# Forgetting attention with its queries, keys, decay and maxima as 16-bit pieces in place of 32-bit ones

## The chip, the cores and the metric

The program runs on 1 core of one Trainium2 chip. The metric is device microseconds (us) of one execution; the time before is the median of 3 runs. A profiled execution is a further run, with a trace of every engine. Engines: PE (TensorE matmul), PEld (its weight loads), DVE (VectorE), ACT (ScalarE), POOL (GpSimd), SP (SyncE, which issues the DMAs).

## The reference

One layer: RMS norm, one input projection, two groups of heads (native sparse attention, NSA, and forgetting attention, FoX), gates, one output projection. There is a prompt of 1024 tokens and a decode batch of 8 x 8 tokens with paged caches. The change touches FoX on the prompt:

```python
def fox_core(q, cq, q_pos, k, v, ck, k_pos):
    s = jnp.einsum('bqhd,bkhd->bhqk', q, k).astype(jnp.float32) * (HEAD_DIM ** -0.5)
    s = s + (jnp.transpose(cq, (0, 2, 1))[:, :, :, None] - jnp.transpose(ck, (0, 2, 1))[:, :, None, :])
    p = masked_softmax(s, k_pos[None, :] <= q_pos[:, None])
    return jnp.einsum('bhqk,bkhd->bqhd', p.astype(v.dtype), v)
```

There are 8 heads of 64. q and k are RMS normed with gains, and c is the running sum of log-forget values over the tokens, so that a score is q.k/8 + c[query] - c[key]. A row's own c[query] falls out of its softmax, so the kernel adds -c[key] alone.

## The kernel before

**Stages.** Prompt tokens are worked in 8 tiles of 128. From 0 to about 366 us the input projection runs chunk after chunk (11 chunks of 256 or so columns, `project`, L237 and L244: 24 matmuls of 128x256 per tile, on 16-bit halves of the input and the weights), with the compression branch, the decay and the operands of FoX head 0 put in as background work at fixed chunks (chunk 6 `nsa_scales`, chunk 8 `fox_decay`, chunk 9 `fox_first`). From 366 us FoX runs over 8 heads, and the last 4 chunks of the projection (36 tiles, kinds `z`) are its filler: after each key block of FoX a quota of 0.48 tiles is let in, until head 6 has had its first half. The second half of head 6 and head 7 run after that, at a raised priority, beside the first loads of the NSA stage and of the decode batch. NSA, the decode batch and the output projection follow.

**FoX on one head h** (buffers of two, i = h % 2):
- `fox_prep(h)`: loads k and q, splits each into a part hi (ACT, L663, rounded to a 32-bit format of TensorE called fp32r) and lo (POOL, L664), transposes both on PE (L669, groups of four 128x128 with `ident`), and copies them out of PSUM (k1 on ACT, L690; q1 on DVE, L693). k1 holds hi over lo, q1 holds lo over hi; the hi halves go by DMA (L694, L695) to rows 0 to 63 of km and qm. Rows 64 and 65 of km hold the decay in two rows (from `cpark`, L685), and qm has ones there.
- `fox_max(h, c)`: row maxima of the scores of one half c of the queries: qm against km over 66 rows (L757), reduced on DVE with the causal mask (L744) or without (L762), into `mst`. `put_max` then transposes the 4 columns of maxima on PE (L722) and writes them, shifted and with a minus, into rows 96 to 99 of qm (DVE, L723), each in its own block of columns.
- `fox_attend(h, c)`: for each key block the score is two matmuls into one PSUM bank (st, two banks): km x qm over 100 rows (L774: hi.hi, decay, minus the maximum) and k1 x q1 over 128 rows (L775: hi.lo and lo.hi). A mask matmul follows on the diagonal (L777). `exp_split` takes exp on ACT (L702, to pf), a 16-bit hi of it on ACT (L705, phi) and the rest lo on DVE, or each fifth time on POOL (L707, plo). `pv` multiplies with the values (L715 to L717), three short matmuls a block of 128 queries.

NSA already works on 16-bit halves: its scores are L1107 and L1108, its exp is L1112 with a bias and a scale read from the tile `nsc`, and its maxima go by `put_max16` (two scaled 16-bit rows each, L732 and L733, one transpose L735, one write L736).

**What sets the order.** A scheduler puts the instructions of each engine in one fixed order when the program is built; each engine then runs its own list in order and waits on semaphores. DMAs are issued by SP in its order.

Of the kernel before, what the change touches and what calls it, by code (L numbers as in the profile page):

```python
# [30 lines left out]
QSCALE = 2.0 ** 10  # L31
TINY = 1e-30
# [55 lines left out]
def bc(ap, shape):  # L88
    return ap.to_broadcast(shape)
# [3 lines left out]
def layer_kernel(ctx, tc, a, o):  # L93
# [15 lines left out]
    nsc = P.tile([128, 8], F32, name="nsc")  # L109
# [7 lines left out]
    gains = P.tile([128, 6, 64], F32, name="gains")  # L117
# [136 lines left out]
    def heads(ap, h):  # L254
        return ap.rearrange("p (h d) -> p h d", h=h)
# [363 lines left out]
    cpark = nc.dram_tensor("cpark", (2, 8, T), F32).ap()  # L619
    km, qm, k1, q1 = [], [], [], []  # L620

    def fox_operands(pool, tags):
        for r, n, tag in zip((km, qm, k1, q1), ("km", "qm", "k1", "q1"), tags):
            r.append(pool.tile([128, T], F32R, name=f"{n}{len(r)}", tag=tag))
        e = nc.gpsimd if pool is C else nc.vector
        e.memset(km[-1][64:96].bitcast(F32), 0.0)
        e.memset(km[-1][96:128].bitcast(F32), 1.0)
        e.memset(qm[-1][64:96].bitcast(F32), 1.0)

    def fox_decay():  # L630
        tri = C.tile([128, 128], F32, name="tri")
        nc.sync.dma_start(tri, a["c_tri"][:, 0:128])
        pc = PS.tile([128, NT, 8], F32, name="ctr", bufs=1)
        nc.tensor.matmul(pc, tri, logf[:, 0:NT], start=True, stop=False)
        for j in range(NT - 1):
            nc.tensor.matmul(pc[:, j + 1:], ones, bc(logf[:, j:j + 1], [128, NT - 1 - j, 8]),
                             start=False, stop=(j == NT - 2))
        nch = C.tile([128, NT, 16], F32R, name="nch")
        nc.scalar.activation(nch[:, :, 0:8], pc, AF.Copy, scale=-1.0)
        nc.vector.scalar_tensor_tensor(nch[:, :, 8:16], pc, -1.0, f32(nch[:, :, 0:8]), op0=ALU.mult, op1=ALU.subtract)  # L640
        for h in range(2):
            p = PS.tile([128, 512], F32, name="ctr", bufs=1)
            for t in range(4):
                nc.tensor.transpose(p[0:16, t * 128:(t + 1) * 128], f32(nch[:, 4 * h + t]), ident)
            cdec = C.tile([16, 512], F32R, name="cdec", tag="ksp", bufs=1)
            nc.scalar.activation(cdec, p[0:16], AF.Copy)
            nc.sync.dma_start(cpark.rearrange("x h t -> (x h) t")[:, 512 * h:512 * h + 512], f32(cdec))
# [35 lines left out]
    def fox_prep(h):  # L683
        i = h % 2
        nc.sync.dma_start(f32(km[i][64:66]), cpark[:, h])  # L685
        for j in range(2):
            c = slice(512 * j, 512 * j + 512)
            ks = C.tile([128, 4, 128], F32R, name="ksp", bufs=1)
            split_heads(kq[h][j][:, :, h % 2], ks[:, :, 0:64], ks[:, :, 64:128])
            nc.scalar.activation(k1[i][:, c], transposed(ks), AF.Copy)  # L690
            qsp = C.tile([128, 4, 128], F32R, name="qsp", bufs=1)
            split_heads(kq[h][2 + j][:, :, h % 2], qsp[:, :, 64:128], qsp[:, :, 0:64])
            nc.vector.tensor_copy(q1[i][:, c], transposed(qsp))  # L693
        nc.sync.dma_start(f32(km[i][0:64]), f32(k1[i][0:64]))  # L694
        nc.sync.dma_start(f32(qm[i][0:64]), f32(q1[i][64:128]))  # L695
# [51 lines left out]
    def fox_max(h, c):  # L747
        i = h % 2
        mst = B2.tile([128, 2, 4], F32, name="mst")
        m = mst[:, c]  # L750
        for x in range(4):
            t = 4 * c + x
            for s in range(c + 1):
                k0, k1_ = 4 * s, min(4 * s + 4, t + 1)
                n = (k1_ - k0) * 128
                p = PM.tile([128, 512], F32, name=bank["smax"][0], bufs=bank["smax"][1])
                nc.tensor.matmul(p[:, :n], qm[i][0:66, t * 128:(t + 1) * 128], km[i][0:66, k0 * 128:k0 * 128 + n],  # L757
                                 start=True, stop=True)
                if s == c:
                    causal_max(p[:, :n], mst[:, 0, x:x + 1] if c else NEG, m[:, x:x + 1])  # L760
                else:
                    nc.vector.tensor_reduce(out=mst[:, s, x:x + 1], in_=p[:, :n], axis=AX.X, op=ALU.max)  # L762
        put_max(m, 96, qm[i], slice(512 * c, 512 * c + 512))

    def fox_attend(h, c):
# [3 lines left out]
        for j in range(last + 1):  # L769
# [4 lines left out]
            nc.tensor.matmul(ps[:, :n], km[i][0:100, j * 128:(j + 1) * 128], qm[i][0:100, cols], start=True, stop=False)  # L774
# [16 lines left out]
    def setup_masks():  # L791
# [17 lines left out]
                  4: [lambda: cmp_cached(2)], 5: [lambda: cmp_cached(3)], 6: [sample_compressed, lambda: nsa_scales()],  # L809
                  7: [setup_masks, finish_gates], 8: [fox_decay, load_logf], 9: [fox_first]}  # L810

    def nsa_scales():

        ab = B.tile([128, 4, 64], F32, name="ropea")
        g = B.tile([128, 4], F32, name="ng", bufs=1)
        for i, k in enumerate((0, 1, 2, 5)):
# [73 lines left out]
    def setup_rows():  # L890
# [3 lines left out]
        nc.scalar.activation(gains.rearrange("p i d -> p (i d)"), p[:, 0:384], AF.Copy)  # L894
# [150 lines left out]
    def nsa_max(g, t, qm):  # L1045
# [34 lines left out]
        put_max16(m.rearrange("p k r -> p (k r)"), 64, qm)  # L1080
# [525 lines left out]
```

## Time and profile before

| | |
|---|---|
| median of 3 runs | 997.69 us |
| lowest and highest | 997.33, 1005.59 us |
| the profiled execution | 998.03 us, of which the span of the trace is 996.3 us |
| PE busy | 926.0 us (93%) |
| DVE, ACT, POOL busy | 636.9 us (64%), 598.2 us (60%), 369.4 us (37%) |
| mean granted clock of PE | 0.979 of full speed |

Busy time of an engine is the time in which the trace has an instruction of it under way. Matmuls overlap, so the recorded length of one is longer than its share of PE: what a matmul costs is read from the start of one to the start of the next. A granted clock of 1.00 is 2.4 GHz and 0.50 is 1.2 GHz.

### The profile page before, as it was taken

What the parts mean: (1) busy time and instruction counts of PE and PEld (TensorE: products, weight loads), DVE (VectorE), ACT (ScalarE), POOL (GpSimd) and SP (SyncE); (2) the same over time, 40 slices, a digit from 0 to 9 for tenths busy, and PEclk for the clock granted to TensorE, in tenths of its full rate; (3) what the DMA queues carried; (4) which work ended last, traced back from release to release, by engine and by line L of the source; (5) the groups of instructions that cost most, each with busy time, mean ns of one, the idle gap of its engine ahead of it and who ended that gap; (6) DMA issues with size and microseconds to landing.
All of it is one profiled execution on the core that took longest, in us unless ns stands there. A gap on an engine that the chain in (4) does not pass through costs nothing.

```text
span 996.3 us, 24627 instructions
## 1 busy us (share of the span) xinstructions
PE 926.0 (93%) x9097; PEld 733.4 (74%) x9097; DVE 636.9 (64%) x1795; ACT 598.2 (60%) x1328; POOL 369.4 (37%) x538
## 2 busy tenths in 40 slices
PE   4799999899999999999998888889999988999997
PEld 3688889779887988888886655666766655677775
DVE  5754666575545325776767546778777899865552
ACT  6844642443444666775766566779887877554530
POOL 4543567664666323242414112333232236420000
PEclk9999999999999999999999779999999999999999
DMA  7563332431243534242215725545344233322431
GB/s 260 139 162 95 100 84 76 115 84 46 84 117 98 137 89 117 73 123 78 81 36 127 227 64 173 172 145 169 128 124 155 83 101 131 109 82 75 117 122 70
DMA packets 122401, 113.88 MB, mean 114 GB/s; under 512 B 39144, under 2 KB 103264, under 8 KB 122256
## 3 DMA queue, kind: packets, MB, share of 16 engines
q1 hardware_dynamic: 121272, 110.65, 37.6%
q0 software_dynamic: 576, 1.05, 0.6%
q8 instruction: 72, 1.18, 0.5%
q10 hardware_dynamic: 432, 0.59, 0.2%
q14 instruction: 49, 0.40, 0.1%
HBM read 79.59 MB, written 27.43 MB: 107 GB/s over the span
## 4 chain that ended last, share of the span: by engine, by line
PE 72%; DMA 9%; ACT 6%; DVE 6%; POOL 3%; issue 3%; SPq 1%; ACTq 0%; POOLq 0%; DVEq 0%
PE acc L244 27%; PE ctr L1492 7%; PE sa L473 3%; PE acc L237 3%; PE st L774 2%; DMA wst<-in_w_in_dram 2%; PE pv L715 2%; PE pv L717 2%; PE pv L716 2%; PE smax L757 2%; PE st L775 2%; PE smax L1063 2%; PE st L1107 2%; PE st L1108 2%; PE tr L669 1%
## 5 line engine op out<-in xcount | busy, mean ns | idle before, releaser
L244 PE MATMUL acc<-wsp,xth 128*128 128x256 f16 (+1 forms) x1920 | 335.8, 275 | 5.4 <-ACT xth L174 3.3
L244 PE MATMUL acc<-wsp,xtl 128*128 128x256 f16 (+1 forms) x960 | 263.9, 275 | 0.0
L244 PEld LDWEIGHTS <-xth 128*128 128x128 f16 x1920 | 186.0, 99 | 34.6 <-issue 6.6
L1112 ACT ACTIVATE pf<-st,nsc 128x512 f32<-128x512 f32 x132 | 98.8, 780 | 43.6 <-PE st L1108 23.0
L244 PEld LDWEIGHTS <-xtl 128*128 128x128 f16 x960 | 94.5, 98 | 15.0 <-issue 3.1
L715 PEld LDWEIGHTS <-phi 128*128 128x128 f16 x816 | 78.0, 98 | 14.5 <-issue 2.6
L717 PEld LDWEIGHTS <-plo 128*128 128x128 f16 x816 | 77.7, 100 | 12.2 <-DVE plo L1115 4.2
L1113 ACT ACTIVATE phi<-pf 128x1024 f16<-128x1024 f32 (+1 forms) x76 | 71.8, 948 | 18.4 <-PE pv L716 13.0
L716 PEld LDWEIGHTS <-phi 128*128 128x128 f16 x816 | 77.9, 99 | 2.6 <-issue 0.5
L263 POOL TENSOR_TENSOR nss<-nss,nhalf 128x4 f32<-128x4 f32 (+3 forms) x72 | 68.3, 950 | 4.8
L1115 DVE TENSOR_TENSOR plo<-pf,phi 128x1024 f16<-128x1024 f32 (+1 forms) x56 | 64.8, 1162 | 5.5 <-ACT phi L1113 3.5
L707 DVE TENSOR_TENSOR plo<-pf,phi 128x512 f16<-128x512 f32 (+3 forms) x77 | 47.8, 628 | 29.4 <-ACT phi L705 27.9
L1115 POOL TENSOR_TENSOR plo<-pf,phi 128x1024 f16<-128x1024 f32 (+1 forms) x20 | 35.8, 1792 | 80.6 <-ACT phi L1113 54.3
L702 ACT ACTIVATE pf<-st 128x512 f32<-128x512 f32 (+1 forms) x96 | 45.3, 487 | 28.9 <-PE st L777 17.6
L715 PE MATMUL pv<-va,phi 128*128 128x65 f16 x528 | 60.1, 194 | 2.0 <-ACT phi L1113 1.1
L716 PE MATMUL pv<-va,phi 128*128 128x64 f16 x528 | 59.8, 196 | 0.0
L717 PE MATMUL pv<-va,plo 128*128 128x65 f16 x528 | 57.4, 193 | 2.0 <-DVE plo L1115 2.0
L200 ACT ACTIVATE vsq<-wst 128x512 f16<-128x512 f32 (+2 forms) x72 | 40.1, 559 | 31.3 <-DMA wst<-in_w_in_dram 30.7
L705 ACT ACTIVATE phi<-pf 128x512 f16<-128x512 f32 (+1 forms) x96 | 49.2, 521 | 14.0 <-PE pv L717 12.4
L1063 PE MATMUL smax<-kma,nqm 88*128 88x512 f16 (+3 forms) x192 | 49.0, 315 | 7.8 <-DVE nm L744 2.8
L744 DVE CUSTOM_DVE_ANT_0 junk<-smax,maskw,nm 128x512 bf16<-128x512 f32 x64 | 47.7, 745 | 8.6 <-PE smax L1063 6.5
L1107 PE MATMUL st<-nqm,kma 88*128 88x512 f16 x132 | 50.6, 383 | 0.6 <-ACT pf L1112 0.5
(445 smaller groups left out, 2405.4 us busy)
## 6 DMA issues: line engine op xcount, KB each, us to landing
wst<-in_w_in_dram SPq DMA_DIRECT2D x56, 256.0 KB
sfk<-in_cache_fox_kv_dram SPq DMA_DIRECT2D x32, 256.0 KB
sfv<-in_cache_fox_kv_dram SPq DMA_DIRECT2D x32, 256.0 KB
out_dram<-kv SPq DMA_DIRECT2D x52, 128.0 KB
xin<-in_x_prompt_dram SPq DMA_DIRECT2D x8, 512.0 KB
cpair<-in_cache_nsa_cmp_kv_dram SPq DMA_DIRECT2D x64, 64.0 KB
zpark<-z SPq DMA_DIRECT2D x32, 128.0 KB
spg<-in_cache_nsa_slc_kv_dram SPq DMA_DIRECT2D x32, 128.0 KB
```

The costliest lines, as they stand in the source:

```text
L244: nc.tensor.matmul(ps[:, :n], x[:, k, t * 128:(t + 1) * 128], w[k // 2][:, i, k % 2, :n], start=(k == 0 and j == 0), stop=(k == KT - 1 and ...
L263: nc.gpsimd.tensor_tensor(ss[:n, 0, :h], ss[:n, 1, :h], nhalf[:n, :h], op=ALU.pow)
L705: nc.scalar.activation(hi[:n, :cols], p[:n, :cols], AF.Copy)
L715: nc.tensor.matmul(po[:, s, 0:65], hi[:, c], v[:, 0:65], start=f, stop=False, skip_group_check=True)
L716: nc.tensor.matmul(po[:, s, 0:64], hi[:, c], v[:, 65:129], start=False, stop=False, skip_group_check=True)
L717: nc.tensor.matmul(po[:, s, 0:65], lo[:, c], v[:, 0:65], start=False, stop=l, skip_group_check=True)
L1063: nc.tensor.matmul(pr[:, r], qm[0:88, (r0 + r) * 128:(r0 + r + 1) * 128], kma[0:88, 2 * k + g, j0 * 128:j1 * 128], start=r == 0, stop=not ...
L1107: nc.tensor.matmul(ps, kma[0:88, 2 * k + g, c], qm[0:88], start=True, stop=False)
L1112: nc.scalar.activation(pf[:, 512 * x:512 * x + 512], ps, AF.Exp, bias=nsc[:, 3:4], scale=nsc[:, 2:3])
L1113: nc.scalar.activation(hi[:, 0:n], pf[:, 0:n], AF.Copy)
L1115: (nc.gpsimd if turn[0] % share[mixed[0]] == 0 else nc.vector).tensor_sub(lo_[:, 0:n], pf[:, 0:n], hi[:, 0:n])
L1492: nc.tensor.matmul(ps, l[:, k], w[:, k, c], start=(k == 0 and j == 0), stop=(k == KT - 1 and j == 2))
```

## The change

1. The FoX operands km, qm, k1 and q1, the split k and q, and the transposes of `fox_prep` become 16-bit (F16), with `ident16`. A matmul on 16-bit operands has a separate LDWEIGHTS instruction in PE's list; one on 32-bit operands loads its weights by itself.
2. So that 16 bits hold them, q gets a gain with a scale in it (`gains[:, 6]`), k is scaled once per two heads on POOL (`kq[h][j]` in place), and the decay is divided by the score's scale, cut off at a floor, and kept as three 16-bit rows (rows 64 to 66).
3. `exp_split` undoes the scale: its exp reads a bias and a scale from `nsc`, as NSA's does.
4. FoX's maxima go the way of NSA's: `put_max16` becomes `put_max` for both, with 8 rows (96 to 103) in qm; the score matmul is over 104 rows, the one of the maxima over 67.
5. `nsa_scales` becomes `score_scales` with 11 more small instructions on DVE.

```diff
-            r.append(pool.tile([128, T], F32R, name=f"{n}{len(r)}", tag=tag))
+            r.append(pool.tile([128, T], F16, name=f"{n}{len(r)}", tag=tag))
...
-        e.memset(km[-1][96:128].bitcast(F32), 1.0)
-        e.memset(qm[-1][64:96].bitcast(F32), 1.0)
+        e.memset(km[-1][96:128], MSCALE)
+        e.memset(qm[-1][64:96], MSCALE)
...
+        lc = C.tile([128, NT, 8], F32, name="lc")
+        nc.vector.tensor_scalar(lc, logf[:, 0:NT], nsc[:, 8:9], None, op0=ALU.max)
...
-        nch = C.tile([128, NT, 16], F32R, name="nch")
-        nc.scalar.activation(nch[:, :, 0:8], pc, AF.Copy, scale=-1.0)
-        nc.vector.scalar_tensor_tensor(nch[:, :, 8:16], pc, -1.0, f32(nch[:, :, 0:8]), op0=ALU.mult, op1=ALU.subtract)
+        x = C.tile([128, NT, 8], F32, name="nch")
+        nh = C.tile([128, NT, 3, 8], F16, name="nch16")
+        nc.scalar.activation(x, pc, AF.Copy, scale=nsc[:, 7:8])
+        for i in range(3):
+            nc.vector.tensor_copy(nh[:, :, i], x)
+            if i < 2:
+                nc.vector.tensor_tensor(x, x, nh[:, :, i], op=ALU.subtract)
...
-        p = PS.tile([128, 4, 128], F32, name=bank["tr"][0], bufs=bank["tr"][1])
+        p = PS.tile([128, 4, 128], F16, name=bank["tr"][0], bufs=bank["tr"][1])
         for t in range(4):
-            nc.tensor.transpose(p[:, t], f32(sc[:, t]), ident)
+            nc.tensor.transpose(p[:, t], sc[:, t], ident16)
...
-        nc.sync.dma_start(f32(km[i][64:66]), cpark[:, h])
+        nc.sync.dma_start(km[i][64:67], cpark[:, h])
         for j in range(2):
             c = slice(512 * j, 512 * j + 512)
-            ks = C.tile([128, 4, 128], F32R, name="ksp", bufs=1)
+            if h % 2 == 0:
+                nc.gpsimd.tensor_scalar(kq[h][j], kq[h][j], nsc[:, 4:5], None, op0=ALU.mult)
+            ks = C.tile([128, 4, 128], F16, name="ksp", bufs=1)
...
-        nc.scalar.activation(p[:n, :cols], ps[:n, :cols], AF.Exp)
+        nc.scalar.activation(p[:n, :cols], ps[:n, :cols], AF.Exp, bias=nsc[:n, 3:4], scale=nsc[:n, 6:7])
...
     def put_max(m, rows, q, cols):
-        n = m.shape[1]
-        p = PM.tile([128, 128], F32, name=bank["smax"][0], bufs=bank["smax"][1])
-        nc.tensor.transpose(p[0:n], m, ident)
-        nc.vector.scalar_tensor_tensor(q[rows:rows + n, cols].rearrange("p (a b) -> p a b", a=4),
-                                       bc(p[0:n, None, :], [n, 4, 128]), -SHIFT,
-                                       block[0:n].rearrange("p (a b) -> p a b", a=4),
-                                       op0=ALU.add, op1=ALU.mult)
-
-    def put_max16(m, rows, q):
         n = m.shape[1]
         mh = B2.tile([128, 2, n], F16, name="mh")
         nc.vector.tensor_scalar(mh[:, 0], m, 1.0 / MSCALE, None, op0=ALU.mult)
         nc.vector.scalar_tensor_tensor(mh[:, 1], m, 1.0 / MSCALE, mh[:, 0], op0=ALU.mult, op1=ALU.subtract)
-        p = PM.tile([128, 128], F16, name="smax", bufs=SMAX)
+        p = PM.tile([128, 128], F16, name=bank["smax"][0], bufs=bank["smax"][1])
         nc.tensor.transpose(p[0:2 * n], mh.rearrange("p x n -> p (x n)"), ident16)
-        nc.vector.tensor_tensor(q[rows:rows + 2 * n].rearrange("p (a b) -> p a b", a=4),
+        nc.vector.tensor_tensor(q[rows:rows + 2 * n, cols].rearrange("p (a b) -> p a b", a=4),
                                 bc(p[0:2 * n, None, :], [2 * n, 4, 128]),
                                 block[0:2 * n].rearrange("p (a b) -> p a b", a=4), op=ALU.mult)
...
-                nc.tensor.matmul(p[:, :n], qm[i][0:66, t * 128:(t + 1) * 128], km[i][0:66, k0 * 128:k0 * 128 + n],
+                nc.tensor.matmul(p[:, :n], qm[i][0:67, t * 128:(t + 1) * 128], km[i][0:67, k0 * 128:k0 * 128 + n],
...
-            nc.tensor.matmul(ps[:, :n], km[i][0:100, j * 128:(j + 1) * 128], qm[i][0:100, cols], start=True, stop=False)
+            nc.tensor.matmul(ps[:, :n], km[i][0:104, j * 128:(j + 1) * 128], qm[i][0:104, cols], start=True, stop=False)
```

The lists of the built programs show where instructions move. First PE at the first maxima of head 7, after the last projection tile. Before: the transpose of the maxima (L722), two matmuls of maxima and the first score block, each 32-bit matmul one row.

```order
L722 MATMUL smax<-ident,mst 4x128
L757 MATMUL smax<-km_5767,qm_5768 128x512
L757 MATMUL smax<-km_5767,qm_5768 128x128
L774 MATMUL st<-qm_5768,km_5767 128x512
L775 MATMUL st<-q_5770,k_5769 128x512
L777 LDWEIGHTS identb
L777 MATMUL st<-maskb,identb 128x128
```

The same place in the changed program (L735 is now the transpose; L726 is what was L717):

```order
L735 LDWEIGHTS mh
L735 MATMUL smax<-ident_62,mh 8x128
L757 LDWEIGHTS qm_5788
L757 MATMUL smax<-km_5787,qm_5788 128x512
L726 LDWEIGHTS plo
L726 MATMUL pv<-vb_5089,plo 128x65
...
L774 LDWEIGHTS km_5787
L774 MATMUL st<-qm_5788,km_5787 128x512
L775 LDWEIGHTS k_5789
L775 MATMUL st<-q_5790,k_5789 128x512
```

The work and its sequence are the same; each weight load is now an instruction of its own in front of its matmul.

Second, DVE where the maxima of the second half of head 6 are written. Before, from the last maximum (L744) to the write (L723), with one subtraction of exp_split (L707) between:

```order
L744 ISA junk,mst<-smax,maskw,mst 128x512
L744 ISA mst 128x1
L707 TENSOR_TENSOR plo<-pf,phi 128x128
L723 SCALAR_TENSOR_TENSOR qm_5244<-smax,block 4x512
```

And in the changed program (L716 is what was L707):

```order
L744 ISA junk,mst<-smax,maskw,mst 128x512
L744 ISA mst 128x1
L732 TENSOR_SCALAR mh<-mst 128x4
L716 TENSOR_TENSOR plo<-pf,phi 128x128
L733 SCALAR_TENSOR_TENSOR mh<-mst,mh 128x4
L736 TENSOR_TENSOR qm_5262<-smax,block 8x512
```

Two small instructions now stand before the transpose, and the subtraction has moved ahead of the second of them, so that PE's transpose waits for it too.

Third, PE at its last projection tile (L237, in the changed program L238). Before, the blocks of the first half of head 6 follow, starting with the one of 512 columns:

```order
L237 LDWEIGHTS xts
L237 MATMUL acc<-wsp,xts 128x256
L757 MATMUL smax<-km_5243,qm_5244 128x128
L774 MATMUL st<-qm_5244,km_5243 128x512
L775 MATMUL st<-q_5246,k_5245 128x512
```

In the changed program the last three blocks of head 5 follow:

```order
L238 MATMUL acc<-wsp,xts 128x256
L676 LDWEIGHTS ksp
L676 MATMUL tr<-ident_62,ksp 128x128
L774 LDWEIGHTS km_5787
L774 MATMUL st<-qm_5788,km_5787 128x384
```

The projection ends three blocks of scores earlier in PE's list: 27 of the 96 blocks stand behind it, where 24 did.

## Rows read from the trace of the kernel before

**Rows 1.** Stretches: start:end, us, then PE, PEld, DVE, ACT, POOL busy, clock, DMA.
```profile
366.00:545.00 179.00, 177.02 (x1917) 149.52 (x1915) 124.35 (x321) 118.14 (x272) 56.18 (x76) 1.00 0.32 86
545.00:592.80 47.80, 40.57 (x332) 28.44 (x332) 25.07 (x62) 29.54 (x72) 10.09 (x13) 0.72 0.55 155
700.00:800.00 100.00, 96.74 (x1225) 66.05 (x1222) 79.78 (x221) 85.69 (x166) 27.46 (x32) 0.98 0.36 114
```

**Rows 2.** PE in order of time, four transposes L669: start us, length us, engine, line.
```profile
370.05 0.27 PE L244 MATMUL acc<-wsp,xtl 128*128 128x256 f16 x1
370.16 0.60 PE L669 MATMUL tr<-ident,ksp 128*128 128x128 f32 x4
370.60 0.38 PE L244 MATMUL acc<-wsp,xth 128*128 128x256 f16 x2
```

**Rows 3.** PE in order of time: first and last undisturbed score pair of 512 columns.
```profile
396.93 0.27 PE L244 MATMUL acc<-wsp,xtl 128*128 128x256 f16 x1
396.96 0.47 PE L774 MATMUL st<-qm,km 100*128 100x512 f32 x1
397.27 0.40 PE L775 MATMUL st<-q,k 128*128 128x512 f32 x1
397.51 0.28 PE L244 MATMUL acc<-wsp,xth 128*128 128x256 f16 x1
...
526.60 0.19 PE L716 MATMUL pv<-vb,phi 128*128 128x64 f16 x1
...
527.18 0.23 PE L777 MATMUL st<-maskb,identb 128*128 128x128 bf16 x1
```

**Rows 4.** PE in order of time: a maxima matmul L757 between projection matmuls.
```profile
372.10 0.27 PE L244 MATMUL acc<-wsp,xth 128*128 128x256 f16 x1
372.13 0.47 PE L757 MATMUL smax<-km,qm 66*128 66x512 f32 x1
372.44 0.28 PE L244 MATMUL acc<-wsp,xth 128*128 128x256 f16 x1
```

**Rows 5.** PE in order of time: NSA's score pair, 16-bit operands.
```profile
639.37 0.38 PE L1107 MATMUL st<-nqm,kma 88*128 88x512 f16 x1
639.59 0.38 PE L1108 MATMUL st<-nq,k1a 128*128 128x512 f16 x1
```

**Rows 6.** Lines L757 and L774 by stretch: us, PE busy (count), PEld busy (count), clock.
```profile
366.00:545.00 179.00, 31.96 (x83) 15.01 (x83) 1.00 0.32 86
366.00:545.00 179.00, 30.65 (x76) 14.62 (x76) 1.00 0.32 86
```

**Rows 7.** PE in order of time at the lower clock, head 6.
```profile
552.24 0.78 PE L774 MATMUL st<-qm,km 100*128 100x512 f32 x1
552.81 0.63 PE L775 MATMUL st<-q,k 128*128 128x512 f32 x1
...
554.09 1.05 PE L669 MATMUL tr<-ident,qsp 128*128 128x128 f32 x4
554.94 0.26 PE L715 MATMUL pv<-vb,phi 128*128 128x65 f16 x1
```

**Rows 8.** Groups by line and shape: xcount | busy us, mean ns | idle before.
```profile
L702 ACT ACTIVATE pf<-st 128x512 f32<-128x512 f32 x48 | 28.1, 594 | 23.1 <-PE st L777 12.3 <-PE st L775 10.2
L1112 ACT ACTIVATE pf<-st,nsc 128x512 f32<-128x512 f32 x132 | 98.8, 780 | 43.6 <-PE st L1108 23.0 <-PE st L1111 9.7 <-DVE plo L1115 6.1
```

**Rows 9.** Groups by line and shape: DVE's steps of put_max and put_max16.
```profile
L723 DVE SCALAR_TENSOR_TENSOR qm<-smax,block 4x512 fp32r<-4x512 f32 x16 | 10.9, 684 | 6.1 <-PE smax L722 4.4 <-PE pv L717 1.4
L736 DVE TENSOR_TENSOR nqm<-smax,block 24x512 f16<-24x512 f16 x16 | 6.7, 416 | 1.0 <-PE smax L735 0.5
L733 DVE SCALAR_TENSOR_TENSOR mh<-nm,mh 128x12 f16<-128x12 f32 x16 | 3.0, 185 | 0.3
```

**Rows 10.** Line L735: what PE sat idle for before it (us, times).
```profile
  DVE mh L733: 3.4, 4
```

**Rows 11.** Groups by line and shape: POOL's multiplication by a column.
```profile
L291 POOL TENSOR_SCALAR rt<-rope,un 128x288 f32<-128x288 f32 x2 | 2.1, 1060 | 0.0
```

More of the change, by code (lines that the diff above doesn't have):

```diff
@@ L108, in layer_kernel @@
     ident16 = P.tile([128, 128], F16, name="ident16")
-    nsc = P.tile([128, 8], F32, name="nsc")
+    nsc = P.tile([128, 10], F32, name="nsc")
     nc.vector.memset(nhalf, -0.5)
@@ L116, in layer_kernel @@
     logf = P.tile([128, 9, 8], F32, name="logf")
-    gains = P.tile([128, 6, 64], F32, name="gains")
+    gains = P.tile([128, 7, 64], F32, name="gains")
     bfb = P.tile([128, 8], F32, name="bfb")
@@ L632, in fox_decay @@
         nc.sync.dma_start(tri, a["c_tri"][:, 0:128])
+        lc = C.tile([128, NT, 8], F32, name="lc")
+        nc.vector.tensor_scalar(lc, logf[:, 0:NT], nsc[:, 8:9], None, op0=ALU.max)
         pc = PS.tile([128, NT, 8], F32, name="ctr", bufs=1)
-        nc.tensor.matmul(pc, tri, logf[:, 0:NT], start=True, stop=False)
+        nc.tensor.matmul(pc, tri, lc, start=True, stop=False)
         for j in range(NT - 1):
-            nc.tensor.matmul(pc[:, j + 1:], ones, bc(logf[:, j:j + 1], [128, NT - 1 - j, 8]),
+            nc.tensor.matmul(pc[:, j + 1:], ones, bc(lc[:, j:j + 1], [128, NT - 1 - j, 8]),
                              start=False, stop=(j == NT - 2))
-        nch = C.tile([128, NT, 16], F32R, name="nch")
-        nc.scalar.activation(nch[:, :, 0:8], pc, AF.Copy, scale=-1.0)
-        nc.vector.scalar_tensor_tensor(nch[:, :, 8:16], pc, -1.0, f32(nch[:, :, 0:8]), op0=ALU.mult, op1=ALU.subtract)
+        x = C.tile([128, NT, 8], F32, name="nch")
[5 more added lines that the diff above has]
+                nc.vector.tensor_tensor(x, x, nh[:, :, i], op=ALU.subtract)
         for h in range(2):
-            p = PS.tile([128, 512], F32, name="ctr", bufs=1)
+            p = PS.tile([128, 512], F16, name="ctr", bufs=1)
             for t in range(4):
[L644 to L647, printed above, removed]
+                nc.tensor.transpose(p[0:24, t * 128:(t + 1) * 128], nh[:, 4 * h + t].rearrange("p x h -> p (x h)"), ident16)
+            cdec = C.tile([24, 512], F16, name="cdec", tag="ksp", bufs=1)
+            nc.scalar.activation(cdec, p[0:24], AF.Copy)
+            nc.sync.dma_start(cpark.rearrange("x h t -> (x h) t")[:, 512 * h:512 * h + 512], cdec)
     lp = P.tile([128, 4, NB, 8], F32, name="slp")
@@ L808, in layer_kernel, with score_scales @@
     background = {1: [cmp_weights, cmp_prompt_tokens], 2: [lambda: cmp_cached(0)], 3: [lambda: cmp_cached(1)],
-                  4: [lambda: cmp_cached(2)], 5: [lambda: cmp_cached(3)], 6: [sample_compressed, lambda: nsa_scales()],
+                  4: [lambda: cmp_cached(2)], 5: [lambda: cmp_cached(3)], 6: [sample_compressed, lambda: score_scales()],
                   7: [setup_masks, finish_gates], 8: [fox_decay, load_logf], 9: [fox_first]}
[L812 to L816, printed above, removed]
+    def score_scales():
+        ab = B.tile([128, 6, 64], F32, name="nab", bufs=1)
+        g = B.tile([128, 6], F32, name="ng", bufs=1)
+        for i, k in enumerate((0, 1, 2, 5, 3, 4)):
             nc.vector.scalar_tensor_tensor(ab[:, i], gains[:, k], -1.0, gains[:, k], op0=ALU.mult, op1=ALU.max)
@@ L819, in nsa_scales @@
         nc.vector.tensor_reduce(out=g[:, 1:2], in_=flat(ab[:, 1:4]), axis=AX.X, op=ALU.max)
+        nc.vector.tensor_reduce(out=g[:, 2:4], in_=ab[:, 4:6], axis=AX.X, op=ALU.max)
         nc.vector.tensor_scalar(g[:, 0:2], g[:, 0:2], 1e-6, 1.0 / QSCALE, op0=ALU.max, op1=ALU.mult)
-        nc.vector.tensor_tensor(nsc[:, 2:3], g[:, 0:1], g[:, 1:2], op=ALU.mult)
+        nc.vector.tensor_scalar(g[:, 2:4], g[:, 2:4], 0.5, 1.0 / FSCALE, op0=ALU.max, op1=ALU.mult)
+        for i in (0, 2):
+            nc.vector.tensor_tensor(nsc[:, 2 * i + 2:2 * i + 3], g[:, i:i + 1], g[:, i + 1:i + 2], op=ALU.mult)
         nc.vector.reciprocal(nsc[:, 0:1], g[:, 1:2])
         nc.vector.reciprocal(nsc[:, 1:2], g[:, 0:1])
+        nc.vector.reciprocal(nsc[:, 4:5], g[:, 3:4])
+        nc.vector.reciprocal(nsc[:, 5:6], g[:, 2:3])
         nc.vector.memset(nsc[:, 3:4], SHIFT)
+        nc.vector.tensor_scalar(g[:, 4:5], nsc[:, 6:7], -MSCALE, None, op0=ALU.mult)
+        nc.vector.reciprocal(nsc[:, 7:8], g[:, 4:5])
+        nc.vector.tensor_scalar(nsc[:, 8:9], nsc[:, 6:7], -2000.0 * FSCALE ** 2, None, op0=ALU.mult)
+        nc.vector.tensor_scalar(gains[:, 6], gains[:, 3], nsc[:, 5:6], None, op0=ALU.mult)
     win_rows = a["cache_nsa_win_kv"][0].rearrange("b t s g d -> b t (s g d)")
@@ L1079, in nsa_max @@
         nc.vector.tensor_reduce(out=m[:, 2], in_=pr, axis=AX.X, op=ALU.max)
-        put_max16(m.rearrange("p k r -> p (k r)"), 64, qm)
+        put_max(m.rearrange("p k r -> p (k r)"), 64, qm, slice(0, 512))
     def nsa_branch(po, k, g, t, oa):
```

17 lines of the change are left out of this document (9 added, 8 removed).

## The prediction

> **What bounds the kernel now.** I first read the page's busy shares: PE is under way 926 of 996.3 us, so a gain has to come out of PE's list, and the question is in which stretch. The table by stretch [rows 1] says it for the two that the change touches. From 366 to 545 us, FoX under its filler, PE has instructions under way in 177.0 of 179 us at a granted clock of 1.00; DVE has 124.4 us (69%), ACT 118.1 (66%), POOL 56.2 (31%). PE alone sets this stretch: about 2.0 us in it are idle. From 545 to 592.8 us, the second half of head 6 and head 7 without filler, PE is under way 40.6 of 47.8 us at a mean clock of 0.72, and a chain through PE, DVE and ACT sets the end.
>
> Then PE's list in order of time, start to start, shows what one instruction costs. 512 columns of 16-bit operands take 0.22 us (639.37 to 639.59, [rows 5]), a projection matmul of 256 columns half of that, 0.11. All 32-bit groups take longer than their columns:
> - Four transposes [rows 2]: from 370.05 to 370.60, less 0.11 for the projection matmul ahead, 0.44 us for 4x128 columns, against 0.22 at the 16-bit pace. Excess 0.22.
> - A score pair [rows 3]: 396.93 to 397.51 less 0.11 is 0.47 against 0.44, excess 0.03 (behind a projection matmul); the last one, 526.60 to 527.18 behind a short pv matmul, excess 0.12 or more. The 18 undisturbed pairs of 512 columns between have a mean of 0.085.
> - A maxima matmul [rows 4]: 372.10 to 372.44 less 0.11 is 0.23, excess 0.01; the others reach 0.12, mean about 0.05.
>
> So columns already go at the full rate, and what 32 bits cost is the weight load in front, which shows more the shorter the work ahead of it. The change buys that load and the transposes, no halving of the scores.
>
> **The sum, dense stretch (366 to 545).** Transposes: 104 of the 128 lie here, 26 groups x 0.22 = 5.7 us. Score pairs: 76 [rows 6]. A 16-bit pair still has a small start of its own; I take 0.07 net, 76 x 0.07 = 5.3. Maxima: 83 [rows 6] x 0.04 net = 3.3. Together -14.3 us. Bounds: nothing below, if a separate weight load is as exposed as the built-in one, and -17.6 above, if every excess goes.
>
> What then is late? With the filler's work unchanged, DVE and ACT have 14 us less to do the same in, and ACT gets more. Its exp now reads a bias and a scale from a tile. The same shape without them takes 594 ns in FoX and with them 780 ns in NSA [rows 8]: +186 ns, 96 times, 17.9 us, 14.1 of it here. ACT rises to 132 of 165 us, 80%, DVE to about 75%. The stretch 700 to 800 us [rows 1] has such loads (ACT 86%, DVE 80%) with PE idle 3.3%: 3.3% of 165 is 5.4 us, less the 2.0 of now, +3.4 for new waits. Bounds: 0, and the rival below.
>
> On ScalarE's exp the Trainium skill ("ScalarE: Activation LUTs", What ACT_TABLE_LOAD costs) speaks against the change: each [128,1] pointer operand adds about 93 ns to an ACTIVATE. The trace agrees, with 186 ns for two.
>
> **fox_first.** Its 4 groups of transposes, under the projection, at 0.22: -0.9.
>
> **The tail (545 to 592.8).** PE runs partly at the lower level, 1.2 GHz, where 512 columns are 0.43 us. There a pair's first matmul takes 552.24 to 552.81 = 0.57, excess 0.14, and four transposes 554.09 to 554.94 = 0.85, excess 0.42 [rows 7]. 8 x 0.14 = 1.1, two groups 0.8, 13 maxima x 0.1 = 1.3: -3.2. Against it: put_max gets two steps of about 185 ns (L733) and its write falls from 684 to 416 ns [rows 9], +0.1 net, three times, +0.3; exp, which follows put_max in the chain, +0.19 at four places, +0.7; and three more blocks stand behind the last projection tile, 27 for 24, now without cover, some 0.5 each by the PE-idle share of this stretch, +1.5. Sum -0.7, bounds -3.2 and +3.
>
> On that write the Trainium skill ("VectorE: DVE Perf Modes", The perf-mode tier table) says that a tensor_tensor with an operand in PSUM runs at 1x, so that 512 16-bit elements from PSUM would gain nothing over 32-bit ones. The trace differs: 416 against 684 ns for the same 512 elements a row [rows 9]. By the page each put_max would cost about 0.25 us more; the sum goes by the row.
>
> **Costed at nothing.** score_scales' 11 small DVE steps at about 185 ns [rows 9], 2.0 us, lie under a chunk of projection matmuls; with that cover gone, +2.0. fox_decay's chain becomes five DVE steps instead of one, some 0.8 us more, but 42 projection matmuls (4.6 us) now stand between its last matmul of sums and its transposes, 25 before; without that, +0.8. POOL scales k eight times: its nearest row is 1060 ns for 288 columns [rows 11], so an estimate of 1.9 us for 512, 15 us in all, on an engine 31% busy [rows 1]. The step stands ahead of the subtraction for lo, so it delays the transposes of every even head's halves; head 0's lies under the projection. The other six would cost up to 1.9 us each, 11 us, if PE had nothing to put before those transposes; it has quotas of projection tiles, and an order that lets prep run a head ahead. put_max in the dense stretch: L733's two steps end 0.4 us later, and PE's transpose behind them holds back what is queued after it (maxima, projection, scores). In NSA PE idled 3.4 us in 4 places for it [rows 10], 0.2 per put_max; 13 such would be 2.6 and are inside the 3.4 above. The DMAs carry half the bytes; none was last.
>
> Total: -14.3 - 0.9 + 3.4 - 0.7 = -12.5. The profiled execution took 998.03, 0.34 above the median of 997.69; 998.03 - 12.5 = 985.5, on the median's footing **985.0 us**.
>
> **Rivals.**
> *ScalarE sets the pace.* st has two banks, so that score j+2 waits for exp j. If PE arrives at each score just as the bank comes free, each exp's 186 ns goes on to PE: 76 x 0.186 = 14.1, the gain is gone, 996 to 997 us. For: ACT at 80%, and its order has NSA's pattern, where exp is last often. Against: ACT is 34% idle, and the filler between two blocks is longer than an exp. 0.25, and beside it 0.03 that a separate load is as exposed as the built-in one, also some 996; the pace of [rows 5] speaks against that.
> *put_max makes PE wait (slower than before).* One mechanism: PE's transpose now follows two small DVE steps, and DVE's order puts a subtraction of exp_split between them (the second fence of the order). A step of 0.33 us, the subtraction up to 0.8, and a second step plus its latency 0.4: 1.5 us in which PE's in-order list stands. At each of 16 that is 24 us, less the 13 gained, +11: 1008 us. It decides from about 0.8 us per put_max on; [rows 10] has 0.2. 0.07.
> *The tail stays at the full clock.* Fewer stalls ahead of 545 us could keep the granted clock at 2.4 GHz. Of the tail some 18 us of PE's work run at the half level; 6 to 9 us would go on top: 976 to 979. Against: the tail has no filler after the change either. 0.12.
>
> **How the numbers follow.** Forecast 0.53, ScalarE or no effect 0.28, put_max 0.07, tail 0.12. NSA behind 592 us is ordered anew by the scheduler, though little of its code is touched; for this I allow 5 us either way. The likeliest case's own range is 978 to 992. The whole range goes from 973 (the dense stretch's upper bound with part of the tail) to 998 (ACT's pace, with 1 us on top), which leaves out the slower rival and the extremes. A measurement of this kernel tells about 1% from no change, 987.7 and 1007.7 us. Faster by more: most of the forecast and the tail, 0.42 + 0.12 = 0.54. Within: 0.11 of the forecast's upper end and the 0.28, 0.39. Slower: 0.07, put_max with the worst of NSA's reordering.
>
> **What would show it.** Right: the last projection tile ends about 11 us earlier with PE still at 98% or so in that stretch; four transposes take 0.22 to 0.25; exp takes 780 ns in FoX. Wrong: PE idle in front of L774 with exp of two blocks earlier as its releaser (ScalarE), or in front of L735 with mh as releaser at more than 0.8 us each (put_max), or ahead of L676 with POOL's subtraction; or 32-bit excess replaced by gaps of the same length behind each LDWEIGHTS.

## The result, and the profile after

The changed kernel takes 988.23 us (median of 15 runs, 983.02 to 996.21) beside 998.99 us for the kernel before on the same chip: a ratio of 0.9879, 95% interval 0.9851 to 0.9908. It is faster by 10.8 us going by the medians and by about 12 us going by the ratio; 985.0 had been forecast, from 973 to 998. Its profiled execution took 983.02 us, the lowest of its runs, with a span of 981.2 us, so that this trace alone makes the gain look larger than it is.

Where the time went, from the starts in PE's list (us). The filler is the last part of the projection, worked between the blocks of FoX. The changed kernel has three traces, two of them from the experiments below:

| | before | changed, three traces |
|---|---|---|
| first projection matmul of the filler starts | 363.0 | 361.2, 361.7, 360.2 |
| last projection matmul starts | 538.5 | 525.4, 526.1, 526.2 |
| last pv matmul of FoX starts | 591.2 | 578.3, 578.7, 580.2 |
| from there to the last matmul | 400.7 | 398.1, 401.6, 398.6 |

The last projection matmul is the last of a row of 16 before, and of a row of 5 after:

```profile
536.83 1.91 PE L237 MATMUL acc<-wsp,xts 128*128 128x256 f16 x16
```
```profile
524.95 0.71 PE L238 MATMUL acc<-wsp,xts 128*128 128x256 f16 x5
```

So the whole gain, 12.2 to 13.1 us, is there by the last projection matmul, the tail of FoX behind it adds nothing, and NSA and what follows take as long as before. In the table by stretch (columns as in [rows 1]) the dense stretch up to that matmul and the tail up to the last pv matmul are, before:

```profile
366.00:538.50 172.50, 171.81 (x1870) 145.68 (x1869) 118.78 (x307) 113.27 (x260) 50.43 (x66) 1.00 0.30 81
538.50:591.20 52.70, 45.61 (x382) 32.23 (x379) 29.13 (x70) 33.06 (x79) 15.12 (x22) 0.74 0.59 164
```

and after:

```profile
366.00:525.40 159.40, 157.14 (x1802) 127.99 (x1800) 115.20 (x322) 119.56 (x252) 56.79 (x72) 1.00 0.28 79
525.40:578.30 52.90, 40.89 (x441) 25.30 (x439) 33.71 (x85) 40.01 (x87) 13.77 (x19) 0.87 0.53 154
```

PE is still under way 98.6% of the dense stretch, at the full clock. ACT is at 75% there (119.56 of 159.40), DVE at 72%. The tail has its PE work done at a mean clock of 0.87, where it was 0.74 before.

What a score pair and four transposes take now, PE in order of time:

```profile
397.91 0.38 PE L774 MATMUL st<-qm,km 104*128 104x512 f16 x1
398.13 0.38 PE L775 MATMUL st<-q,k 128*128 128x512 f16 x1
398.35 0.22 PE L777 MATMUL st<-maskb,identb 128*128 128x128 bf16 x1
398.40 0.39 PE L676 MATMUL tr<-ident,qsp 128*128 128x128 f16 x4
398.62 0.27 PE L245 MATMUL acc<-wsp,xth 128*128 128x256 f16 x1
```

The pair takes 397.91 to 398.35, 0.44 us, behind a pv matmul of 65 columns, where [rows 3] had it dearest. Four transposes take 398.40 to 398.62, 0.22, for the 0.44 of [rows 2]. In these rows nothing is left above the columns.

FoX's exp, and the four longest waits of PE from 525 to 580 us (line waited for: total us, times, longest), the latter in the second trace of the changed kernel:

```profile
L711 ACT ACTIVATE pf<-st,nsc 128x512 f32<-128x512 f32 x48 | 36.8, 775 | 12.3 <-PE st L777 4.0 <-PE st L775 3.9 <-DVE plo L716 2.6
```
```profile
PE smax L735 <- DVE mh L733: 5.3, 1, 5.3
PE pv L726 <- DVE plo L716: 1.9, 6, 0.5
PE st L774 <- ACT pf L711: 1.5, 4, 0.4
PE pv L724 <- ACT phi L714: 1.0, 2, 0.8
```

Exp has become 181 ns longer, near the 186 of [rows 8], and PE waits for it 1.5 us in four places. But one wait of 5.3 us is new: PE stands in front of a transpose of the maxima (L735). It is in all three traces of this program, and the next section is largely about it. In the first trace it looks like this on PE:

```profile
530.91 0.22 PE L777 MATMUL st<-maskb,identb 128*128 128x128 bf16 x1
536.38 0.27 PE L735 MATMUL smax<-ident,mh 128*8 128x128 f16 x1 [5.25 <-DVE mh L733]
```

on DVE:

```profile
530.48 0.68 DVE L762 TENSOR_REDUCE mst<-smax 128x1 f32<-128x512 f32 x1
531.08 4.10 DVE L716 TENSOR_TENSOR plo<-pf,phi 128x256 f16<-128x256 f32 x1
535.10 0.74 DVE L744 CUSTOM_DVE_ANT_0 junk<-smax,maskw,mst 128x512 bf16<-128x512 f32 x1
...
535.88 0.17 DVE L732 TENSOR_SCALAR mh<-mst 128x4 f16<-128x4 f32 x1
535.96 0.28 DVE L716 TENSOR_TENSOR plo<-pf,phi 128x128 f16<-128x128 f32 x1
536.16 0.16 DVE L733 SCALAR_TENSOR_TENSOR mh<-mst,mh 128x4 f16<-128x4 f32 x1
```

and on POOL:

```profile
530.83 0.92 POOL L716 TENSOR_TENSOR plo<-pf,phi 128x384 f16<-128x384 f32 x1
531.70 0.67 POOL L671 TENSOR_TENSOR ksp<-kql,ksp 128x256 f16<-128x256 f32 x1
532.31 0.24 POOL L1248 MEMSET spr<- 128x64 f32 x2
532.50 0.66 POOL L671 TENSOR_TENSOR qsp<-kql,qsp 128x256 f16<-128x256 f32 x1
533.13 1.14 POOL L1021 TENSOR_TENSOR nqs<-nq,nqs 128x512 f16<-128x512 f32 x1
534.24 0.66 POOL L1021 TENSOR_TENSOR nks<-kn,nks 128x256 f16<-128x256 f32 x1
```

put_max's two steps are short, 0.17 and 0.16. The long one is a subtraction of exp_split in front of them: 4.10 us for 256 columns, and it ends 0.3 us after the last of five POOL subtractions, which ran one behind the other with only two short memsets between.

### The profile page after: what moved, and what is told of

Same layout as the page of the kernel before. It is cut to its first block, busy times and chain, and to the rows that moved or that the text cites. A ratio compares the mean times of both kernels' runs of the same rounds, so it can differ in the third digit from the quotient of the medians.

```text
span 981.2 us, 24638 instructions
## 1 busy us (share of the span) xinstructions
PE 907.3 (92%) x9097; PEld 709.6 (72%) x9097; DVE 636.7 (65%) x1843; ACT 611.9 (62%) x1328; POOL 383.7 (39%) x546
## 4 chain that ended last, share of the span: by engine, by line
PE 68%; DVE 8%; DMA 7%; ACT 5%; issue 3%; POOL 3%; SPq 1%; ACTq 0%; DVEq 0%; POOLq 0%
PE acc L245 25%; PE ctr L1502 7%; PE sa L474 3%; PE acc L238 3%; PE pv L724 2%; PE pv L726 2%; PE pv L725 2%; PE st L1117 2%; PE smax L1073 2%; PE st L1118 2%; DMA wst<-in_w_in_dram 2%; PE smax L757 1%; PE st L774 1%; PE ctr L1550 1%; PE st L775 1%
## 5 line engine op out<-in xcount | busy, mean ns | idle before, releaser
L726 PEld LDWEIGHTS <-plo 128*128 128x128 f16 x816 | 77.2, 100 | 11.5 <-DVE plo L716 2.9
L711 ACT ACTIVATE pf<-st,nsc 128x512 f32<-128x512 f32 (+1 forms) x96 | 62.9, 669 | 16.0 <-PE st L777 5.8
L716 DVE TENSOR_TENSOR plo<-pf,phi 128x512 f16<-128x512 f32 (+3 forms) x77 | 51.9, 680 | 22.2 <-ACT phi L714 20.3
L726 PE MATMUL pv<-va,plo 128*128 128x65 f16 x528 | 57.5, 193 | 0.2 <-POOL plo L1125 0.2
L744 DVE CUSTOM_DVE_ANT_0 junk<-smax,maskw,nm 128x512 bf16<-128x512 f32 x64 | 47.7, 746 | 6.3 <-PE smax L1073 4.1
```

The source lines that it names most:

```text
L711: nc.scalar.activation(p[:n, :cols], ps[:n, :cols], AF.Exp, bias=nsc[:n, 3:4], scale=nsc[:n, 6:7])
L726: nc.tensor.matmul(po[:, s, 0:65], lo[:, c], v[:, 0:65], start=False, stop=l, skip_group_check=True)
```

## The experiments

Each was timed against the kernel before on its chip. Where a number says "changed", it is the changed kernel: 0.9879, and in two repeats 0.9904 and 0.9871.

**Which operands gave the gain.** First the kernel before, with 16-bit transposes alone.

```diff
-            ks = C.tile([128, 4, 128], F32R, name="ksp", bufs=1)
+            ks = C.tile([128, 4, 128], F16, name="ksp", bufs=1)
...
-            nc.tensor.transpose(p[:, t], f32(sc[:, t]), ident)
+            nc.tensor.transpose(p[:, t], sc[:, t], ident16)
```

> The kernel before with only the split k and q and their transposes in 16 bits (km, qm, k1, q1, decay, maxima, exp as before; k and q unscaled, so that the lo parts lose digits). Exposed weight loads: 32 groups of four transposes lose 0.22 us each (0.42 in the two of the tail), 7.4 us, so about 0.7% faster than before, each group 0.22 to 0.25 us in the trace. Rival, that other engines hold the pace as soon as PE gets faster: under 2 us. The fox_decay stage stays as it was, with its two waits for the ACT copy of 1.4 us each; if the 3 us that the changed kernel gains ahead of 366 us come from there, none of it shows here beyond the 0.9 of fox_first.

Measured: 0.9936 (0.9906 to 0.9966), about 6.4 us. Four transposes take 0.22 us now:

```profile
371.22 0.39 PE L669 MATMUL tr<-ident,ksp 128*128 128x128 f16 x4
371.44 0.38 PE L244 MATMUL acc<-wsp,xth 128*128 128x256 f16 x2
```

As expected: 7.4 us had been worked out. The wait of fox_decay's transposes for the ACT copy, 1.4 us, is still there (the second wait there, 1.3 us, is for a DVE step and not for ACT); in every trace with the new fox_decay it is gone, though in three of them a wait of 1.4 to 1.8 us for a DVE step stands in its place.

Then its complement, the changed kernel with 32-bit transposes.

```diff
-            ks = C.tile([128, 4, 128], F16, name="ksp", bufs=1)
+            ks = C.tile([128, 4, 128], F32R, name="ksp", bufs=1)
...
-            nc.tensor.transpose(p[:, t], sc[:, t], ident16)
+            nc.tensor.transpose(p[:, t], f32(sc[:, t]), ident)
```

> The changed kernel with the transposes back at 32 bits (split k and q in fp32r, PSUM in F32; the copies to k1 and q1 round to 16 bits). The complement of the run before: exposed weight loads expect it 5 to 7 us slower than the changed kernel, so 0.4 to 0.7% faster than before, with four transposes at 0.44 us. If instead the loads of scores and maxima carry nothing, it is level with the kernel before; if the transposes carry nothing, level with the changed one.

Measured: 0.9931 (0.9907 to 0.9956), about 6.9 us faster than before, with four transposes at 0.44 us (375.54 to 375.98 in its trace). The two halves add up within their intervals of 0.3% each: 0.64% and 0.69%, against 1.21% for the whole. Both terms are real, and no other engine took back a gain of this size as PE became faster.

For the transposes the rows leave open whether it is the weight load that costs. In [rows 2] the first of the four starts 0.11 us after the projection matmul ahead, as one more projection matmul would, so that no load shows in front of it; each of the four then takes 0.11 us, the last one too, behind which a 16-bit load follows. Columns that pass at half the pace in a 32-bit transpose would give the same starts, and no run here tells the two apart. For the scores that rival is out: a 32-bit pair takes 0.47 to 0.56 us for the 0.44 of a 16-bit one, where half the pace would make it 0.88.

**Does exp set the pace?** The changed kernel without the bias and with a constant scale in FoX's exp; the shift and the factor of the gains are left out.

```diff
-        nc.scalar.activation(p[:n, :cols], ps[:n, :cols], AF.Exp, bias=nsc[:n, 3:4], scale=nsc[:n, 6:7])
+        nc.scalar.activation(p[:n, :cols], ps[:n, :cols], AF.Exp, scale=1.0 / FSCALE ** 2)
```

> The changed kernel with exp's bias left out and its scale an immediate number in FoX (the shift and the factor of the gains are left out). Exp of 512 columns goes back from 775 ns to about 594. Theory that ACT's extra 17 us are mostly covered: 1 to 3 us faster than the changed kernel, the waits of the scores for exp (2.6 us in its trace from 363 to 580 us) less by about 2. Rival, ScalarE sets the pace: 8 to 14 us faster.

Measured: 0.9876 (0.9851 to 0.9902), level with the changed kernel. Exp of 512 columns is back at 592 ns, and the time did not move. The rival in which ScalarE sets the pace is out; the 1 to 3 us of the other theory are below what this measurement resolves.

**Do put_max's steps or POOL's scaling cost time?** FoX's maxima in one row each, without the low rows, the score over 100 rows:

```diff
-        put_max(m, 96, qm[i], slice(512 * c, 512 * c + 512))
+        put_one(m, 96, qm[i], slice(512 * c, 512 * c + 512))
```

> The changed kernel with FoX's maxima in one row each again (transposed in 32 bits, written once as 16 bits; the low rows and the two small steps are left out). Theory that put_max's two steps cost something only where DVE is held, in the tail: 0 to 4 us faster than the changed kernel, the waits for L735 gone, others in their place. Rival, that the two steps make PE wait at each of 16: 8 us or more faster.

and without POOL's scaling of k:

```diff
-            if h % 2 == 0:
-                nc.gpsimd.tensor_scalar(kq[h][j], kq[h][j], nsc[:, 4:5], None, op0=ALU.mult)
```

> The changed kernel without POOL's scaling of k (8 steps of 1.58 us, left out). Theory that it lies under the filler: within 2 us of the changed kernel. Rival, that it delays the transposes of the even heads: 5 to 11 us faster.

Measured: 0.9865 (0.9818 to 0.9912) and 0.9855 (0.9806 to 0.9903), beside 0.9904 (0.9869 to 0.9940) for the changed kernel in the same series. Each may be worth 4 or 5 us or nothing, since the intervals overlap that of the changed kernel, and the times alone do not exclude the lower ends of the two rivals. As waits of PE the trace of the changed kernel excludes both: of the 16 put_max of FoX only one has PE waiting in front of L735 (5.2 us), and in front of the transposes of the heads (L676) PE has no wait that POOL ends.

**The wait of 5 us: is POOL its cause?** First, the four POOL subtractions of that moment (head 7's second halves, NSA's first queries and keys) go to DVE.

```diff
-        nc.gpsimd.tensor_sub(lo, src, hi)
+        e.tensor_sub(lo, src, hi)
```

> The changed kernel with the POOL subtractions that ran from 531 to 535 us (lo of the second halves of head 7, and lo of NSA's first queries and keys) on DVE. Theory, that DVE's subtraction of exp_split took 4.10 us in place of 0.42 because POOL read SBUF at the same time and that PE waited 5.2 us for the maxima behind it: that subtraction back to 0.4 to 0.6 us, PE's wait for mh down to 1 to 2 us, 2 to 4 us faster than the changed kernel. Rival, that the wait is the chain's own (maxima, two small steps, transpose) and POOL stands beside it by chance: the wait stays at 4 to 5 us and the time within 1 us.

Measured: 0.9915 (0.9884 to 0.9947). The subtraction takes 0.63 us and the wait for mh is gone from that place, but the kernel is not the 2 to 4 us faster that were expected: PE now waits 1.5 us there for the moved subtraction (qsp), 2.0 us for another put_max at 564 us, and the stages after FoX, in another order, are 10 us longer than in the first trace of the changed kernel.

Since moving work also moves the order, the next run keeps DVE's order at this place. The four steps stay on POOL, as memsets, which write and do not read; these lo parts are left out. POOL's own order did move: three of the four memsets ran earlier (at 528.6, 530.2 and 533.5 us), one stands beside DVE's step.

```diff
-        nc.gpsimd.tensor_sub(lo, src, hi)
+        if zero:
+            nc.gpsimd.memset(lo, 0.0)
+        else:
+            nc.gpsimd.tensor_sub(lo, src, hi)
```

> The changed kernel with the same four POOL steps (lo of the second halves of head 7, lo of NSA's first queries and keys) as memsets, which read nothing; these lo parts are left out. DVE's order at the maxima of head 6 is that of the changed kernel. Theory, that DVE's step with two SBUF operands stands still as long as POOL reads SBUF: the subtraction of 256 columns goes from 4.10 us to 0.4 to 1.3 (one POOL subtraction of exp_split is left beside it), PE's wait for mh from 5.2 to about 2 us. Rival, that the step was held by something else (its own wait, or POOL being busy at all): it stays near 4 us. Time: 2 to 4 us faster than the changed kernel, if what follows in the tail takes it up; the run before, with these steps on DVE, lost the stall but was not faster.

DVE, PE and POOL at the same place (L719 is exp_split's subtraction here):

```profile
536.58 1.23 DVE L719 TENSOR_TENSOR plo<-pf,phi 128x256 f16<-128x256 f32 x1
537.73 0.74 DVE L747 CUSTOM_DVE_ANT_0 junk<-smax,maskw,mst 128x512 bf16<-128x512 f32 x1
```
```profile
539.00 0.27 PE L738 MATMUL smax<-ident,mh 128*8 128x128 f16 x1 [2.14 <-DVE mh L736]
```
```profile
536.59 0.93 POOL L719 TENSOR_TENSOR plo<-pf,phi 128x384 f16<-128x384 f32 x1
537.45 0.32 POOL L672 MEMSET qsp<- 128x256 f16 x1
```

Same step, same place in the list: 1.23 us beside the one POOL subtraction that is left, and PE's wait falls from 5.25 to 2.14. In each of these traces the subtraction of 256 columns ends 0.28 or 0.29 us behind the last POOL subtraction beside it: at 535.18 for 534.90 in the changed kernel, here at 537.81 for 537.52, while POOL had gone on to memsets. So it is POOL's subtractions that hold DVE, and the memsets behind the last of them do not. The time: 0.9889 (0.9844 to 0.9934), again not faster. The profiled execution was the slowest of the eight (996.01, median 988.40), and its tail took 55.3 us, 2.4 more than with the wait, at a lower clock:

```profile
530.90:586.20 55.30, 45.71 (x442) 28.44 (x439) 29.82 (x86) 40.38 (x87) 12.00 (x19) 0.75 0.51 149
```

PE is under way 45.7 us at 0.75, for the 40.9 us at 0.87 of the changed kernel.

Is the wait of fixed length? The changed kernel once more:

> The changed kernel once more, unaltered, for a second trace and the spread of its runs. Time 0.988 of before, within 0.3%. If the wait of 5 us for mh at the start of the tail comes from a fixed order of instructions, it is there again at the same place, 4 to 6 us long; if it was chance, it is not.

It is: 4.11 us for the subtraction and 5.25 for PE. In other orders of the list another DVE step is caught: without the scaling, L731, the second step of put_max, on 128x4 elements.

```profile
529.80 3.90 DVE L731 SCALAR_TENSOR_TENSOR mh<-mst,mh 128x4 f16<-128x4 f32 x1
```

**A version without POOL in the operands.** k's scale goes into the split: hi on ACT with the scale, lo on DVE as one multiply and subtract. The whole computation is kept.

```diff
-            nc.gpsimd.tensor_sub(lo, src, hi)
+            nc.scalar.activation(hi, src, AF.Copy, scale=s)
+            nc.vector.scalar_tensor_tensor(lo, src, s, hi, op0=ALU.mult, op1=ALU.subtract)
```

> The changed kernel with k's scale taken into the split itself: hi by ACT with the scale, lo on DVE as one multiply and subtract, so that POOL's 8 scalings (12.6 us) and 16 of its subtractions (11.3 us) go and DVE gets 16 steps of about 0.42 us (6.7 us). The whole computation is kept. If the steps of POOL cost time by holding DVE in the dense stretch, 2 to 4 us faster than the changed kernel; if both lie under PE's filler, within 1.5 us of it; if DVE at 72% has no room, 3 us slower or more.

Measured: 0.9837 (0.9797 to 0.9876). That is 4 to 7 us under the changed kernel (0.9879 and 0.9904), more than expected, so it was run again, beside the changed kernel and beside a version with q's lo on DVE as well.

> The changed kernel, beside the next two on the same chip: 0.988 to 0.990 of before.

> The version with k's scale and lo on DVE again: if its gain is real, 0.982 to 0.986 of before and 4 us or more under the changed kernel of this series; if the first measurement was luck of the chip, 0.988.

> The same with q's lo on DVE as well, so that no POOL step of the operands is left (16 more DVE steps of 0.42 us, 16 subtractions fewer on POOL). If POOL beside DVE is what costs, another 0 to 3 us faster; if DVE has no room left, 2 us or more slower than the one before.

```diff
         if s is None:
             nc.scalar.activation(hi, src, AF.Copy)
-            nc.gpsimd.tensor_sub(lo, src, hi)
+            nc.vector.tensor_sub(lo, src, hi)
```

Measured side by side: the changed kernel 0.9871 (0.9837 to 0.9905), k's lo on DVE 0.9804 (0.9761 to 0.9847), both on DVE 0.9766 (0.9730 to 0.9802), medians 986.25, 981.37 and 979.01 us. k's lo on DVE gains a little more than expected; what q's adds, 2.4 us, is not resolved, since the intervals of these two overlap. The last one beats both kernels, by 2.3% the one before and by some 1.1% the changed one (0.9766 / 0.9871), with intervals that do not meet. Its stretches to the last projection tile and to the end of FoX, and its subtraction of 256 columns, then that of the changed kernel of this series:

```profile
366.00:523.80 157.80, 157.53 (x1819) 129.14 (x1819) 119.70 (x350) 122.18 (x256) 32.78 (x44) 1.00 0.29 81
523.80:574.30 50.50, 40.47 (x425) 24.86 (x422) 30.54 (x85) 38.45 (x83) 12.89 (x17) 0.83 0.52 156
```
```profile
L718 DVE TENSOR_TENSOR plo<-pf,phi 128x256 f16<-128x256 f32 x12 | 5.0, 417 | 1.2 <-ACT phi L716 1.2
```
```profile
L716 DVE TENSOR_TENSOR plo<-pf,phi 128x256 f16<-128x256 f32 x12 | 10.0, 829 | 1.4 <-ACT phi L714 1.4
```

POOL is busy 32.8 us in the dense stretch for 57.1, the subtractions of 256 columns on DVE have a mean of 417 ns for 829 (of whose 10.0 us one instruction had 4.1), PE is idle 0.3 us in the dense stretch, and FoX ends at 574.3 us for 580.2; from there to the last matmul this trace, the slowest execution of its six, takes 402.5 us for 398.6. DVE took 32 steps more and is still at 76%. That taking POOL out of the operands brings time is shown. That all of it comes by DVE steps that are no longer held is not: the order of the lists moved with it, and the two runs in which only the long wait was taken away gained nothing.

## Why the prediction was right, point by point

**The dense stretch.** Forecast: -14.3 us of weight loads and transposes, of which 13.4 lie ahead of the last projection matmul of the kernel before (24 groups of transposes, 72 pairs, 77 maxima), +3.4 of new waits, and -0.9 ahead of the stretch. From the first projection matmul of the filler to the last it is 175.5 us before and 164.2, 164.4 and 166.0 after. At 0.218 us for 512 columns [rows 5], 156.8 us of these are columns before and 154.6 after. PE is idle 0.7 us before and 3.0 to 3.2 after. What is left, the excess of loads and transposes, goes from 18.0 to 6.6, 6.6 and 8.2 us (in the third trace the clock falls to its lower level for 3.4 us). So the excess fell by 11.4 in two traces and 9.8 in the third, and waits grew by some 2.4: both terms were taken somewhat large, in opposite directions. The 2.2 us of columns are work of the three score blocks that moved behind the last projection matmul, which the sum had not taken out of this stretch. With the 1.3 to 2.8 us already gained ahead of the filler, the last projection matmul came 12.2 to 13.1 us earlier, a little more than the "about 11" that was to be the sign. That the load of a 16-bit score or maxima matmul is hidden where a built-in one shows is what the run with 32-bit transposes and the pair of 0.44 us say; that the transposes cost by their load is not shown. The prediction's bound of -17.6 is also too wide: its own means (26 x 0.22, 76 x 0.085, 83 x 0.05) give 16.3. And 985.5 less 0.34 is 985.2 and not 985.0.

**exp.** +181 ns each, for 186; ACT at 75%, for 80%. The longer exp is covered by other work, and without it the time is the same. The price that the prediction took from the Trainium skill ("ScalarE: Activation LUTs", What ACT_TABLE_LOAD costs), about 93 ns for each pointer operand, agrees, and had no effect on the time here.

**put_max.** The forecast had 0.2 us for each and, as the slower rival, 1.5 us at each of 16. One of the 16 took 5.25, the others next to nothing. What the rival named is there, PE's list standing behind a put_max while DVE works through a subtraction of exp_split; but the subtraction between the two small steps took 0.28 us. The one that was held is another, in front of the last maximum, which the rival did not have in its chain, and it took 4.1 where the rival allowed up to 0.8.

**The tail.** -0.7 forecast; from the last projection matmul to the last pv it took 52.7 us before and 52.9, 52.6 and 53.9 after. That is near the forecast, and right by accident: things that were not in the sum cancel. PE is idle 7.1 us of the tail before and 12.0 to 13.7 after, most of the difference in the one wait of 5 us, and it has the 2.2 us of columns more to do; against that, it ran less at the lower level. From 545.7 to 555.5 and from 568 to 586 us before, 27.8 us in all, and after in two stretches of 15.7 us:

```profile
545.70:555.50 9.80, 7.63 (x42) 5.73 (x42) 4.96 (x11) 5.78 (x12) 3.14 (x4) 0.52 0.90 244
568.00:586.00 18.00, 16.87 (x114) 11.78 (x114) 9.66 (x22) 11.80 (x29) 4.25 (x4) 0.53 0.17 46
```
```profile
533.60:542.00 8.40, 5.39 (x56) 3.62 (x57) 5.52 (x13) 5.26 (x10) 1.96 (x3) 0.59 0.52 142
561.70:569.00 7.30, 6.72 (x48) 3.66 (x49) 3.38 (x11) 4.70 (x13) 0.53 (x1) 0.53 0.17 46
```

0.52 to 0.59 is the level of 1.2 GHz with some time of 2.4 at the edges. The first low stretch begins around a wait of PE in both: one of 1.8 us before the change (to 545.7, for phi), and one of 5.25 us after it (to 536.4, for mh). So the rival of a faster tail came half true, and the slower rival at one place.

**Costed at nothing.** For score_scales and the memsets PE has no wait; for a DMA of q's hi halves into qm it has one of 0.4 us in the dense stretch. fox_decay gave up a wait of 1.4 us in place of costing: its ACT copy no longer stands behind three ACT steps that wait for weights. The POOL scaling took 1.58 us a step for the 1.9 of the estimate. What the sum had not seen is that POOL's work costs DVE's time, though POOL itself is busy a third of the stretch.

## What to carry to other kernels

Where PE sets the pace, as in this dense stretch, what 32-bit operands cost is their time above the columns; read it start to start in PE's list, and it can be added up instruction by instruction (13.4 us by the forecast, 9.8 to 11.4 measured). When two traces are compared by stage, take the same instruction as the mark in both, and ask what work has moved across it. POOL, a third busy, was not free to give work to: its subtractions held DVE for up to 4.1 us. Look for single instructions far longer than others of their form, and see what the neighbour did meanwhile. And a wait that is taken out of a stage that runs at a changing clock need not come back as time; here two runs without it were no faster, while taking POOL out of the operands everywhere was worth 1%.

## What the runs showed of the hardware that was not expected

A DVE step with two operands in SBUF stood still not for one POOL instruction, but for five in a row: 4.10 us, where the last version has a mean of 0.42, and across two memsets of POOL that lay between them. The Trainium skill ("SBUF — State Buffer", Who interferes with whom) says that a DVE instruction with two SBUF inputs contends with a GpSimd instruction that reads SBUF and not with one that only writes. This agrees with the run with memsets (1.23 us). Of DVE's two-port modes the same section says that whoever issues first has the shared ports for the whole instruction and the other fully blocks. In length the traces go further: here DVE did not get its turn between one POOL instruction and the next, in all three traces of the program. Nor is it only a step with two operands that is caught: in the run with 32-bit transposes L732, which reads the maxima alone, took 2.98 us beside three POOL subtractions, for 0.17.

The clock of the tail is not the same in two executions of one program. The version with k's lo on DVE was profiled twice; its tails, from about the last projection matmul to the last pv of FoX:

```profile
522.40:569.40 47.00, 38.16 (x429) 24.66 (x426) 29.23 (x84) 38.60 (x84) 13.24 (x18) 0.85 0.57 168
```
```profile
524.70:577.40 52.70, 43.41 (x427) 27.05 (x424) 29.06 (x84) 38.75 (x84) 13.25 (x18) 0.74 0.51 150
```

The same instructions, 47.0 us at 0.85 and 52.7 at 0.74. In the 15 runs of the changed kernel too, the five with a mean clock of 0.982 or more took 983.0 to 985.5 us and the four with 0.974 or less 989.1 to 996.2. A single trace says little on a gain of 5 us in such a stage.
